# Moving the halves of weights and activations to other byte remainders in a two-block transformer kernel

## The chip, the cores and the metric

The kernel runs on one core of a Trainium2 chip. The metric is the device time of one execution in microseconds (us); the profile is one such execution. The engines are named as in the profile: PE is the matrix engine (its weight loads are listed apart as PEld), DVE the vector engine, ACT the scalar engine, POOL GpSimd, and SP the engine that issues most transfers.

## The reference

Two blocks follow each other on one sequence of 256 tokens with 1024 channels; block 1 has a context of another 256 tokens beside it.

```python
# block 1, two layers: x and ctx
x = sandwich_ffn(x, ...); ctx = sandwich_ffn(ctx, ...)      # gate/up 1024 -> 2 x 2816, silu, down
out_x, out_c = token_mix(hx, hc, w_in, w_out, ...)          # attention + pooling
x = x + gate * rms_norm(out_x); ctx likewise
x = sandwich_ffn(x, ...); ctx = sandwich_ffn(ctx, ...)      # no ctx in the last layer's second half
# block 2, four layers: mixers gla, mla, conv, gla
h = mixer(x)
x = layer_norm(ALPHA * x + h)
x = layer_norm(ALPHA * x + square(relu(x @ w1)) @ w2)       # 1024 -> 4096 -> 1024
x = x + sigmoid(x @ ple_w_gate) * (p @ ple_w_proj)
```

Everything is float32.

## The kernel before

**Products.** Each float32 operand is split exactly into two float32r halves, hi and lo. `mm3` forms one product of two split operands by three matmuls (L180, L181, L182: hi hi, then hi lo, lo hi). `halves` (from L161) makes the halves of weights: the raw weights of a transfer (tile `raw`, 128 x 2048, three buffers) go through one ACT copy (L169, `whi`) and one DVE subtraction (L170, `wlo`), 128 x 1024 at a time, into rings of four buffers each. `split` (L174, L175) does the same for activations.

There are two ways to multiply. `gemm_rows` keeps 128 x 128 activations stationary and moves weights of 512 columns (down projections, `mix_in`, `mix_out`, `mlp` second half, `m_out`, `ple`). `gemm_cols` keeps 128 x 128 weights stationary and moves the activations of all tokens: 512 columns where x and ctx are worked together (`ffn` with `ns == 2`, three of the four feed-forwards of block 1), 256 columns where there is x alone (`ffn` with `ns == 1`, the last feed-forward of block 1; `mlp_hidden`, `gla`'s `project` and `conv` in block 2). Each weight half of 1024 columns serves eight blocks of 128, so 24 matmuls in a row read the same pair of buffers. In the feed-forwards with `ns == 2` the first four pairs are taken over 256 columns at a time.

**Order.** The engines work in the order in which the code emits instructions, moved by priorities (`sooner`, `later`). Transfers of weights go out on SP's queue, three ahead. Steps that form the modulation vectors (`mod_units`, DVE sums) are emitted between the products of the feed-forwards.

**Places in memory.** All tiles lie in the on-chip memory behind each other: pools in the order in which they are opened, tags in the order of first use, each buffer rounded up to 32 bytes. An address here is the byte offset within a partition; its remainder by 512 is what the change speaks of.

| tile | first byte | remainder by 512 |
|---|---|---|
| `whi`, four buffers of 4096 bytes | 51808 | 96, each |
| `wlo`, four buffers of 4096 bytes | 68192 | 96, each |
| block 1: `hT_hi`, `hT_lo` (and `pcat`) | 96992, 113376 | 224 |
| block 1: `hid_hi`, `hid_lo` | 168672, 191200 | 224 |
| block 2: `xT_hi`, `xT_lo`, two buffers each | 84576, 92768, 100960, 109152 | 96 |
| block 2: `mlp_hi`, `mlp_lo` | 159328, 192096 | 96 |
| block 2, mla alone: `cT_hi`, `cT_lo` | 162592, 166688 | 288 |

A block of 128 weights is 512 bytes, a row of 256 columns 1024, a row of 512 columns 2048. So every slice that a matmul of 128 x 128 weights reads has its tile's remainder. One product differs: in mla a weight of 64 columns (`wk`) has slices 256 bytes apart, so its slices stand at 96 and 352 in turn, against `xT` at 96. [...]

**The start.** `rows` (three small transfers) is transposed to `cols`; ACT writes silu of it into `sil`, 128 x 8 x 32 with zeros beyond the first two columns, which is the stationary operand of the first products of the modulation (L323, `mod_pair`). The DVE sums take single columns of `sil` as scalars.

Of the kernel before, what the change touches and what calls it, by code (L numbers as in the profile page):

```python
# [18 lines left out]
P = 128  # L19
# [4 lines left out]
SOONER = 60  # L24
DFF2 = 4096
# [11 lines left out]
def _constants():  # L37
    """Arrays that depend on shapes alone."""
    c = {}
    c["ident"] = np.eye(P, dtype=np.float32)  # L40
    c["one_col"] = np.repeat(np.array([0, 1], np.float32), 64)[:, None]
    inv = np.float32(10000.0) ** (-np.arange(16, dtype=np.float32) / np.float32(16))
    t = np.arange(256)
    tab = np.zeros((2, 2, 256, 2, 16), np.float32)
    for half, pos in enumerate((t // 64, t % 64)):
        ang = pos.astype(np.float32)[:, None] * inv
        tab[0, 0, :, half] = np.cos(ang)
        tab[0, 1, :, half] = np.sin(ang)
    tab[1] = tab[0]
    tab[0] *= np.float32(0.125)  # L50
    c["rope"] = np.ascontiguousarray(
        tab.reshape(2, 2, 2, P, 32).transpose(3, 0, 2, 1, 4).reshape(P, 256))
    j = np.arange(64)
    start = np.clip(j - 8, 0, 48)
    ok = (j[None] >= start[:, None]) & (j[None] < start[:, None] + 16)
    c["na_mask"] = np.tile(np.where(ok, 0.0, NEG).astype(np.float32), (2, 1))

    def pool_matrix(n):
        out = []
        for w in (2, 4, 8, 16):  # L60
            i = np.arange(n)
            lo = np.clip(i - w // 2, 0, n)
            hi = np.clip(i - w // 2 + w, 0, n)
            a = ((i[None] >= lo[:, None]) & (i[None] < hi[:, None])) / (hi - lo)[:, None] - np.eye(n)
            out.append(a.T)
        return np.array(out, np.float32)

    a64 = pool_matrix(64)
    ax = np.zeros((4, P, P), np.float32)
    ax[:, :64, :64] = a64  # L70
    ax[:, 64:, 64:] = a64
    c["pool_x"] = np.ascontiguousarray(ax.transpose(1, 0, 2).reshape(P, 512))
    c["pool_c"] = np.ascontiguousarray(
        pool_matrix(256).reshape(4, 2, P, 256).transpose(2, 1, 0, 3).reshape(P, 2048))
    s = np.arange(P)
    mats, masks = [], [np.eye(P, dtype=bool)]
    for b in (2, 4, 8, 16, 32, 64, 128):
        blk = s // b
        mid = blk * b + b // 2
        up = s >= mid  # L80
        m = np.zeros((P, P), bool)
        for tt in range(P):
            if up[tt]:
                m[mid[tt]:tt + 1, tt] = True
            else:
                m[tt + 1:mid[tt], tt] = True
        mats.append(m)
        if b < 64:
            masks.append((blk[:, None] == blk[None]) & (up[:, None] != up[None]))
    mats.insert(0, s[:, None] > s[None])  # L90
    mats.append(s[:, None] <= s[None])
    c["gla_lev"] = np.concatenate(mats, axis=1).astype(np.float32) / np.float32(16)
    c["gla_mask"] = np.tile(np.concatenate([m[:64, :64] for m in masks], axis=1).astype(np.int32), (2, 1))
    inv2 = np.float32(10000.0) ** (-np.arange(0, 32, dtype=np.float32) * np.float32(2.0 / 64))
    c["mla_inv"] = np.tile(inv2.astype(np.float32), (P, 1))
    return c


class Net:
# [38 lines left out]
    def fbank(self):  # L138
        """Either kind of bank in turn."""
        self.turn = not self.turn  # L140
        return self.bank() if self.turn else self.xbank()
# [19 lines left out]
    def halves(self, v, shape=None, tag=""):  # L161
        """The exact split of v into two float32r parts."""
        kn, cn = v.shape[1], v.shape[2]
        out = []
        for nm in ("hi", "lo"):
            t = self.w.tile([P, 1024], F32R, tag="w" + nm + tag, name="w" + nm, bufs=self.SPL)
            out.append(t[:, :kn * cn].rearrange("p (k c) -> p k c", k=kn))
        hi, lo = out
        self.nc.scalar.copy(hi, v)  # L169
        self.nc.vector.tensor_sub(lo, v, hi.bitcast(F32))  # L170
        return hi, lo
# [5 lines left out]
    def mm3(self, ps, a, b, first, last):  # L177
        """ps += a^T b with both as (hi, lo) pairs."""
# [5 lines left out]
    def gemm_cols(self, ps, w, x, c0, cn):  # L184
        """ps[feature, token] over all k: w hi/lo [P, k, 128], x hi/lo [P, k, tokens]."""
# [5 lines left out]
    def gemm_rows(self, w, kn, c0, cn, x, tiles, per=4, major=2, order=None, bank=None):  # L191
        """Banks [token, column] for each tile; w is a DRAM matrix with kn k-tiles.

        The last major loads are taken tile by tile, so that the first tiles end early."""
# [23 lines left out]
    def rstd_of(self, ms, eps):  # L218
        """(ms + eps)^-1/2; eps may be a column."""
# [10 lines left out]
    def rstd_of_two(self, ms):  # L230
        """The same from the two halves' mean squares."""
# [4 lines left out]
    def meansq(self, src, n):  # L236
        """The sum of squares over n, a power of four."""
# [5 lines left out]
    def columns(self, rows, n, pool, name):  # L243
        """[n, 128] rows -> [128, n]."""
# [6 lines left out]
    def to_columns(self, rows, hi, lo, c0, nblk):  # L251
        """rows: list of tiles [P, nblk*128]; hi/lo [P, block, token] at c0 get the transposes."""
# [13 lines left out]
    def block1(self):  # L266
        nc, tc, d = self.nc, self.tc, self.d
        with ExitStack() as ctx:
# [6 lines left out]
            rows = self.act.tile([24, P], F32, name="rows")  # L275
# [5 lines left out]
            self.sil = self.act.tile([P, KD, 32], F32, name="sil")  # L281
            nc.vector.memset(self.sil, 0.0)
            for s in range(2):
                nc.scalar.activation(self.sil[:, :, s], cols[:, 8 * s:8 * s + 8], AF.Silu)
            self.one_col = self.load_const("one_col", self.act)
# [8 lines left out]
            self.na_mask = self.load_const("na_mask", self.act)  # L294
            self.tail = None
# [13 lines left out]
    def mod_raw(self, l, v, k0):  # L309
        """Rows of k-tiles k0, k0+1 for vector v."""  # L310
# [3 lines left out]
    def mod_pair(self, l, v):  # L314
        """Vectors v and v+1 by matrix products; bank rows 32j (x) and 32j+1 (ctx) for half j."""
# [3 lines left out]
        for k in range(KD):  # L319
            raw = self.load(self.d["w_mod"][l, k * P:(k + 1) * P, v * D:(v + 2) * D]  # L320
                            .rearrange("p (o c) -> p o c", o=1), 1, 2 * D)
            for j in range(4):
                nc.tensor.matmul(acc[32 * j:32 * j + 32, :], lhsT=self.sil[:, k, :],  # L323
# [7 lines left out]
    def mod_units(self, l, vectors):  # L331
        """Steps that form the vectors by sums on the vector engine over k, then over partitions."""
# [36 lines left out]
    def mod_finish(self, l, acc, rows):  # L369
        """From the bank rows (row, vector, half, stream): + b_mod, (1 + scale) g, gate g."""  # L370
# [44 lines left out]
    def modulated(self, l, i, groups):  # L415
        """hT hi/lo [P, 8, tokens] of the modulated norm i for groups of token tiles, each after its tail."""
# [38 lines left out]
    def sooner(self, on=True):  # L455
        """Puts a chain that others wait for ahead of the products around it."""
        return self.tc.high_priority(offset=SOONER) if on else ExitStack()

    def later(self, by):
        """Lets products fill what the chains emitted after them leave free."""  # L460
        return self.tc.high_priority(offset=-by)

    def add_normed(self, t, y, ms):
        """x += y * rstd, y already times the gate row."""
# [4 lines left out]
    def ffn(self, l, w, ns):  # L469
# [25 lines left out]
        with self.tc.tile_pool(name="hid", bufs=1) as hp:  # L495
            self.hp = hp
            for part in range(2):
                hid = tuple(hp.tile([P, HALF_F, 512], F32R, tag="h" + nm, name="hid_" + nm) for nm in ("hi", "lo"))
                for f0 in range(0, HALF_F, 2):
# [7 lines left out]
                    work = [(self.fbank(), h) for h in pre or self.gate_up(l, w, part * HALF_F + f0, fn)]  # L507
# [36 lines left out]
    def gate_up_rows(self, l, w, hT, hid):  # L544
        """Blocks 0 and 1 token by token, so that tile 0 goes ahead."""
# [17 lines left out]
    def gate_up(self, l, w, f0, fn):  # L563
        """The split gate and up columns of blocks f0..f0+fn, in turn."""
        wgu = self.d["w_ffn_gate_up"][l, w]
        raws = [self.load_cols(wgu, c + f0 * P, fn * P) for c in (0, DFF)]
        return [self.halves(r[:, :, f * P:(f + 1) * P]) for f in range(fn) for r in raws]
# [94 lines left out]
    def stacks(self, hp, mp, q, k):  # L662
        """Heads 2hp and 2hp+1 on partitions: q as (hi, lo), (lo, hi) and k as hi twice; k's lo parts in place."""
# [26 lines left out]
    def attend(self, l, s, hp, mp, stacks, vu, cat):  # L690
        """Heads 2hp and 2hp+1 of stream s: local and context keys for x, context keys for ctx."""
# [30 lines left out]
    def softmax_T(self, sc, nk, scale, mp, dst):  # L722
        """Softmax over the free axis of sc, transposed in blocks into dst [P, nk, 128]."""
# [19 lines left out]
    def na_bias(self, l, hp, t, mp):  # L743
        """[P queries, head, 256 keys]: rpb laid out over the window, -1e30 outside it."""
# [78 lines left out]
    def rows_to_xT(self, t, b0, b1, x):  # L823
        """Blocks b0..b1 of token tile t into x."""
# [16 lines left out]
    def layer_norm(self, i, j, gemm):  # L841
        """x = norm(ALPHA x + gemm); returns x transposed, hi/lo."""
# [29 lines left out]
    def mlp_hidden(self, i, hp, x):  # L872
        """relu(x w1)^2 transposed, hi/lo; the first columns token by token, so that tile 0 goes ahead."""
# [13 lines left out]
        for f in range(4, 32, 2):  # L887
            raw = self.load_cols(d["mlp_w1_2"][i], f * P, 256)
            ps = self.bank()
            for e in range(2):  # L890
                w = self.halves(raw[:, :, e * P:(e + 1) * P])
# [4 lines left out]
    def ple_in(self, i):  # L896
        """The transposed per-layer input, hi/lo."""
# [13 lines left out]
    def ple(self, i, pe, x, last):  # L911
        """x += sigmoid(x w) * pe; returns the new x transposed, or stores it."""
# [18 lines left out]
    def gla(self, j, mp, x):  # L931
# [27 lines left out]
        def project(c):  # L959
            raw = self.load_cols(w_in, 256 * c, 256)  # L960
            ps = self.bank()
            for e in range(2):
                self.gemm_cols(ps[:, e * 256:e * 256 + 256], self.halves(raw[:, :, e * P:(e + 1) * P]), x, 0, 256)
# [28 lines left out]
        def scores(h):  # L992
            """Decayed scores of head h [key, query] within each tile and across the two."""
# [102 lines left out]
    def rotate(self, dst, src, cs, t, nh, mp):  # L1096
        """dst, src [P, nh*64]."""
# [14 lines left out]
    def mla(self, j, mp, x):  # L1112
# [23 lines left out]
        def rope_key():  # L1136
            """The rotated key part of all heads, twice over the partitions."""
# [23 lines left out]
        def up(raws, off, width):  # L1161
            """hi/lo [P, 8 heads, width] of the head columns at off, for both k-tiles."""
# [41 lines left out]
        def scores(h):  # L1204
            """The softmax of head h, keys on partitions."""
# [41 lines left out]
    def conv(self, j, mp, x):  # L1247
# [6 lines left out]
        for f0 in range(0, KD, 2):  # L1254
            raws = [self.load_cols(w_in, D * e + f0 * P, 256) for e in range(3)]
            for f in range(2):
                fb = f0 + f
                ps = []
                for e in range(3):
                    b = self.bank()  # L1260
                    self.gemm_cols(b[:, :256], self.halves(raws[e][:, :, f * P:(f + 1) * P]), x, 0, 256)
# [56 lines left out]
```

## Time and profile before

| | |
|---|---|
| median of three runs | 3044.11 us (3041.87 to 3045.15) |
| profiled execution, span | 3045.1 us |
| PE busy | 2980.0 us, 98% |
| DVE busy | 1875.6 us, 62% |
| ACT busy | 1281.8 us, 42% |
| instructions | 40666 |

The span runs from the first to the last instruction. A matmul's duration in the trace is longer than the distance from its start to the next one's start, since matmuls are pipelined: what a matmul costs is read from starts, or from how many fall into a stretch.

### The profile page before, as it was taken

The numbers are of one execution on the slowest core, as the hardware profiler recorded it, in microseconds if no ns is written. First come the engines' busy times: TensorE is split into PE (matmuls) and PEld (weight loads), VectorE is DVE, ScalarE is ACT, GpSimd is POOL, SyncE is SP. The second block draws the span as 40 slices with busy tenths as digits, with TensorE's granted clock in tenths as the row PEclk, the third lists the DMA queues.
The fourth block names the chain that finished last, engine by engine and source line by source line (L and its number), as shares of the span: only waits on it lengthen the run. The fifth ranks groups of instructions, "written<-read, shape, count | busy, mean of one in ns | idle before, by whom it ended". The sixth has DMA issues, their size and how long they took to land.

```text
span 3045.1 us, 40666 instructions
## 1 busy us (share of the span) xinstructions
PE 2980.0 (98%) x16362; PEld 2481.3 (81%) x16362; DVE 1875.6 (62%) x2454; ACT 1281.8 (42%) x1876; POOL 288.6 (9%) x480
## 2 busy tenths in 40 slices
PE   7999999999999999999999999999999999999999
PEld 5777777787778877787789888987798989887997
DVE  5757765577553775336655567656664776467755
ACT  3222245442222422224654465546453545355543
POOL 2101030011110110001100121000000000002000
PEclk9999999999999999999999999999999999999999
DMA  7555531245543454333345536554455565553654
GB/s 280 179 175 180 187 107 63 91 155 180 170 132 110 149 181 154 99 98 120 97 160 186 176 130 192 187 181 165 131 184 187 183 201 183 186 194 111 198 180 145
DMA packets 321936, 484.70 MB, mean 159 GB/s; under 512 B 16606, under 2 KB 199442, under 8 KB 320340
## 3 DMA queue, kind: packets, MB, share of 16 engines
q1 hardware_dynamic: 307844, 461.75, 46.2%
q0 software_dynamic: 9296, 16.16, 1.6%
q10 hardware_dynamic: 4608, 4.20, 0.5%
q8 instruction: 128, 2.10, 0.3%
q14 instruction: 60, 0.49, 0.0%
HBM read 480.97 MB, written 1.10 MB: 158 GB/s over the span
## 4 chain that ended last, share of the span: by engine, by line
PE 89%; DVE 5%; POOL 2%; ACT 2%; DMA 1%; issue 1%; SPq 0%; ACTq 0%; DVEq 0%; POOLq 0%
PE ffn_gu L180 9%; PE ffn_gu L182 9%; PE ffn_gu L181 9%; PE mlp L181 7%; PE mlp L180 7%; PE mlp L182 7%; PE ffn_dn L182 4%; PE ffn_dn L181 4%; PE ffn_dn L180 4%; PE m L180 3%; PE m L182 3%; PE m L181 3%; DVE wlo L170 2%; PE mix_in L181 1%; PE mix_in L180 1%; PE mix_in L182 1%
## 5 line engine op out<-in xcount | busy, mean ns | idle before, releaser
L170 DVE TENSOR_TENSOR wlo<-raw,whi 128x1024 fp32r<-128x1024 f32 (+1 forms) x735 | 884.9, 1211 | 636.6 <-ACT whi L169 621.6
L169 ACT CAST whi<-raw 128x1024 fp32r<-128x1024 f32 (+1 forms) x735 | 760.7, 1038 | 1129.9 <-PE ffn_gu L181 290.7
L181 PE MATMUL ffn_gu<-hT_lo,whi 128*128 128x512 f32 (+1 forms) x1472 | 524.5, 357 | 1.8 <-DVE hT_lo L175 1.8
L180 PE MATMUL ffn_gu<-hT_hi,whi 128*128 128x512 f32 (+1 forms) x1472 | 525.7, 358 | 0.5 <-ACT hT_hi L174 0.5
L182 PE MATMUL ffn_gu<-hT_hi,wlo 128*128 128x512 f32 (+1 forms) x1472 | 523.8, 356 | 0.7 <-DVE wlo L170 0.7
L180 PEld LDWEIGHTS ffn_gu<-hT_hi,whi 128*128 128x128 f32 x1472 | 277.7, 189 | 52.9 <-ACT whi L169 4.2
L181 PEld LDWEIGHTS ffn_gu<-hT_lo,whi 128*128 128x128 f32 x1472 | 278.1, 189 | 43.8 <-DVE hT_lo L175 2.4
L182 PEld LDWEIGHTS ffn_gu<-hT_hi,wlo 128*128 128x128 f32 x1472 | 277.8, 189 | 43.7 <-DVE wlo L170 1.3
L347 DVE SCALAR_TENSOR_TENSOR macc<-raw,sil,macc 128x1024 f32<-128x1024 f32 x224 | 274.6, 1277 | 42.9 <-DMA raw<-in_w_mod_dram 42.9
L180 PE MATMUL mlp<-xT_hi,whi 128*128 128x256 f32 x896 | 253.9, 283 | 0.0
L181 PE MATMUL mlp<-xT_lo,whi 128*128 128x256 f32 x896 | 253.8, 283 | 0.0
L182 PE MATMUL mlp<-xT_hi,wlo 128*128 128x256 f32 x896 | 253.5, 283 | 0.0
L180 PE MATMUL ffn_dn<-whi,hid_hi 128*128 128x512 f32 x616 | 244.1, 396 | 0.0
L181 PE MATMUL ffn_dn<-wlo,hid_hi 128*128 128x512 f32 x616 | 243.6, 395 | 0.0
L182 PE MATMUL ffn_dn<-whi,hid_lo 128*128 128x512 f32 x616 | 243.5, 395 | 0.0
L180 PE MATMUL mlp<-whi,mlp_hi 128*128 128x512 f32 x512 | 199.2, 389 | 0.0
L181 PE MATMUL mlp<-wlo,mlp_hi 128*128 128x512 f32 x512 | 199.2, 389 | 0.0
L182 PE MATMUL mlp<-whi,mlp_lo 128*128 128x512 f32 x512 | 199.2, 389 | 0.0
L181 PEld LDWEIGHTS mlp<-xT_lo,whi 128*128 128x128 f32 x896 | 172.0, 192 | 0.0
L182 PEld LDWEIGHTS mlp<-xT_hi,wlo 128*128 128x128 f32 x896 | 172.0, 192 | 0.0
L180 PEld LDWEIGHTS mlp<-xT_hi,whi 128*128 128x128 f32 x896 | 172.0, 192 | 0.0
L180 PEld LDWEIGHTS ffn_dn<-whi,hid_hi 128*128 128x128 f32 x616 | 115.9, 188 | 29.3 <-ACT yrow L489 2.5
(402 smaller groups left out, 4794.5 us busy)
## 6 DMA issues: line engine op xcount, KB each, us to landing
raw<-in_mlp_w_dram SPq DMA_DIRECT2D x128, 1024.0 KB, 5.4
raw<-in_w_ffn_gate_up_dram SPq DMA_DIRECT2D x80, 1024.0 KB, 5.3
raw<-in_w_mod_dram SPq DMA_DIRECT2D x72, 1024.0 KB, 5.2
raw<-in_w_ffn_down_dram SPq DMA_DIRECT2D x32, 1024.0 KB, 5.1
raw<-in_gla_w_in_dram SPq DMA_DIRECT2D x24, 1024.0 KB, 5.2
raw<-in_w_in_dram SPq DMA_DIRECT2D x16, 1024.0 KB, 5.0
raw<-in_ple_w_gate_dram SPq DMA_DIRECT2D x16, 1024.0 KB, 5.2
raw<-in_w_ffn_down_dram SPq DMA_DIRECT2D x16, 768.0 KB, 4.6
```

The source lines that it names most:

```text
L169: self.nc.scalar.copy(hi, v)
L170: self.nc.vector.tensor_sub(lo, v, hi.bitcast(F32))
L180: mm(ps, lhsT=a[0], rhs=b[0], start=first, stop=False)
L181: mm(ps, lhsT=a[0], rhs=b[1], start=False, stop=False)
L182: mm(ps, lhsT=a[1], rhs=b[0], start=False, stop=last)
L347: nc.vector.scalar_tensor_tensor(acc[s], raw[:, k - k0, :], c, acc[s], ALU.mult, ALU.add)
```

## The change

- `halves` allocates tiles of 1024 + 64 columns in place of 1024. Each buffer of `whi` and `wlo` is 256 bytes longer, so the four buffers of a ring start at remainders 96, 352, 96, 352; both rings turn together. The optional parameters `shape` and `tag`, which no call used, go; a parameter `skew` comes, by which the halves start that many elements into the tile.
- `SKEW = 16` elements, 64 bytes, is given in the `gemm_cols` products with 256 columns of `ffn` with `ns == 1`, `mlp_hidden`, `gla`'s `project`, and `conv`. There the weights start at remainder 160 or 416.
- `rows` goes from the pool `act` into a buffer of `tmp`; `sil` shrinks to 128 x 8 x 2, and its wide form with zeros is a buffer of `tmp` (`gp`), filled by a DVE copy. Together with `even(80)`, a tile of 320 bytes that POOL fills with zeros, this moves `hT` to 97888 and 114272 and `hid` to 169568 and 192096: remainder 96. Block 2's tiles move by 2048 bytes and keep their remainders. The highest byte in use becomes 228960.

Comments and docstrings are emptied throughout; those lines are left out here.

```diff
+SKEW = 16
...
+    def even(self, n):
+        self.nc.gpsimd.memset(self.act.tile([P, n], F32, name="even"), 0.0)
...
-    def halves(self, v, shape=None, tag=""):
+    def halves(self, v, skew=0):
         kn, cn = v.shape[1], v.shape[2]
         out = []
         for nm in ("hi", "lo"):
-            t = self.w.tile([P, 1024], F32R, tag="w" + nm + tag, name="w" + nm, bufs=self.SPL)
-            out.append(t[:, :kn * cn].rearrange("p (k c) -> p k c", k=kn))
+            t = self.w.tile([P, 1024 + 64], F32R, tag="w" + nm, name="w" + nm, bufs=self.SPL)
+            out.append(t[:, skew:skew + kn * cn].rearrange("p (k c) -> p k c", k=kn))
...
-            rows = self.act.tile([24, P], F32, name="rows")
+            rows = self.tmp.tile([P, 512], F32, tag="hf", name="rows", bufs=3)[:24, :P]
...
-            self.sil = self.act.tile([P, KD, 32], F32, name="sil")
-            nc.vector.memset(self.sil, 0.0)
+            self.sil = self.act.tile([P, KD, 2], F32, name="sil")
+            wide = self.tmp.tile([P, D], F32, tag="gp", name="wide")
+            self.wide = wide[:, :KD * 32].rearrange("p (k s) -> p k s", k=KD)
+            nc.vector.memset(self.wide, 0.0)
             for s in range(2):
                 nc.scalar.activation(self.sil[:, :, s], cols[:, 8 * s:8 * s + 8], AF.Silu)
+            nc.vector.tensor_copy(self.wide[:, :, 0:2], self.sil)
...
             self.na_mask = self.load_const("na_mask", self.act)
+            self.even(80)
...
-                nc.tensor.matmul(acc[32 * j:32 * j + 32, :], lhsT=self.sil[:, k, :],
+                nc.tensor.matmul(acc[32 * j:32 * j + 32, :], lhsT=self.wide[:, k, :],
...
-                    work = [(self.fbank(), h) for h in pre or self.gate_up(l, w, part * HALF_F + f0, fn)]
+                    work = [(self.fbank(), h) for h in pre or self.gate_up(l, w, part * HALF_F + f0, fn,
+                                                                           SKEW if ns == 1 else 0)]
...
-        return [self.halves(r[:, :, f * P:(f + 1) * P]) for f in range(fn) for r in raws]
+        return [self.halves(r[:, :, f * P:(f + 1) * P], skew) for f in range(fn) for r in raws]
...
-                w = self.halves(raw[:, :, e * P:(e + 1) * P])
+                w = self.halves(raw[:, :, e * P:(e + 1) * P], SKEW)
```

The same third argument is added in `project` of `gla` and in `conv`.

## Rows read from the trace of the kernel before

**Rows 1.** The page: busy time, granted clock by slices, the chain that ended last.
```profile
PE 2980.0 (98%) x16362; PEld 2481.3 (81%) x16362; DVE 1875.6 (62%) x2454; ACT 1281.8 (42%) x1876; POOL 288.6 (9%) x480
...
PEclk9999999999999999999999999999999999999999
...
PE 89%; DVE 5%; POOL 2%; ACT 2%; DMA 1%; issue 1%; SPq 0%; ACTq 0%; DVEq 0%; POOLq 0%
```

**Rows 2.** Waits of PE, longest in total first: us, times, longest.
```profile
PE mod L323 <- DMA raw<-in_w_mod_dram: 11.8, 8, 2.9
PE ffn_t L440 <- DVE yrow L428: 6.8, 8, 1.7
```

**Rows 3.** Matmuls by line and shape: count | busy us, mean ns.
```profile
L180 PE MATMUL ffn_gu<-hT_hi,whi 128*128 128x512 f32 x960 | 380.3, 396 | 0.0
...
L180 PE MATMUL mlp<-xT_hi,whi 128*128 128x256 f32 x896 | 253.9, 283 | 0.0
...
L180 PE MATMUL ffn_dn<-whi,hid_hi 128*128 128x512 f32 x616 | 244.1, 396 | 0.0
...
L180 PE MATMUL mlp<-whi,mlp_hi 128*128 128x512 f32 x512 | 199.2, 389 | 0.0
...
L180 PE MATMUL ffn_gu<-hT_hi,whi 128*128 128x256 f32 x512 | 145.4, 285 | 0.5 <-ACT hT_hi L174 0.5
...
L180 PE MATMUL m<-xT_hi,whi 128*128 128x256 f32 x320 | 91.5, 287 | 1.1 <-ACT whi L169 1.1
...
L180 PE MATMUL mix_in<-whi,hT_hi 128*128 128x512 f32 x224 | 89.9, 407 | 0.0
...
L180 PE MATMUL mix_out<-whi,pcat_hi 128*128 128x512 f32 x84 | 34.0, 405 | 0.0
```

**Rows 4.** Stretches of one kind of matmul: us, busy time of each engine (count), clock, DMA.
```profile
1230.00:1330.00 100.00, 100.00 (x432) 81.06 (x431) 33.55 (x36) 28.31 (x36) 1.92 (x4) 1.00 0.33 102
1340.00:1390.00 50.00, 50.00 (x216) 40.23 (x215) 19.15 (x22) 12.95 (x23) 6.78 (x11) 1.00 0.24 82
1640.00:1697.00 57.00, 57.00 (x483) 57.00 (x482) 32.72 (x41) 26.96 (x40) 0.00 (x0) 1.00 0.61 199
1965.00:2047.00 82.00, 82.00 (x364) 67.91 (x363) 40.89 (x40) 31.17 (x30) 0.62 (x1) 1.00 0.56 186
1886.00:1962.00 76.00, 76.00 (x636) 76.00 (x635) 47.76 (x52) 40.62 (x53) 0.00 (x0) 1.00 0.58 183
2400.00:2460.00 60.00, 60.00 (x503) 60.00 (x502) 42.87 (x70) 26.41 (x36) 0.00 (x0) 1.00 0.60 197
2108.60:2112.40 3.80, 3.80 (x36) 3.80 (x35) 3.80 (x10) 1.87 (x4) 0.00 (x0) 1.00 0.00 0
2091.30:2093.30 2.00, 2.00 (x20) 2.00 (x19) 1.23 (x2) 0.68 (x3) 1.49 (x2) 1.00 0.74 311
```

**Rows 5.** PE in order of time, block 1, first feed-forward: start us, duration us.
```profile
100.29 0.40 PE L181 MATMUL ffn_gu<-hT_lo,whi 128*128 128x512 f32 x1
100.53 0.40 PE L182 MATMUL ffn_gu<-hT_hi,wlo 128*128 128x512 f32 x1
100.77 0.39 PE L180 MATMUL ffn_gu<-hT_hi,whi 128*128 128x512 f32 x1
```

**Rows 6.** PE in order of time, mla's values in block 2, first and last of eleven.
```profile
2104.21 0.39 PE L180 MATMUL m<-whi,cT_hi 128*128 128x512 f32 x1
...
2106.49 0.39 PE L181 MATMUL m<-wlo,cT_hi 128*128 128x512 f32 x1
```

**Rows 7.** All engines in order of time, the start.
```profile
4.09 0.18 DVE L248 COPY cols<-init_t 128x24 f32<-128x24 f32 x1 [2.93 <-PE init_t L246]
4.31 0.31 ACT L284 ACTIVATE sil<-cols 128x8 f32<-128x8 f32 x2 [2.29 <-DVE cols L248]
...
6.95 1.93 PE L323 MATMUL mod<-raw,sil 128*32 128x512 f32 x8 [2.90 <-DMA raw<-in_w_mod_dram]
```

**Rows 8.** Transposes on PE by line and shape, in block 1 and in block 2.
```profile
L740 PE MATMUL mix_att_t<-ident,pr 128*128 128x128 f32 x160 | 25.4, 276 | 0.0
...
L828 PE MATMUL m_out_t<-ident,xr 128*128 128x128 f32 x64 | 9.2, 276 | 1.2 <-DVE xr L868 1.1
```

More of the change, by code (lines that the diff above doesn't have):

```diff
@@ L561, in gate_up_rows, with gate_up @@
             self.to_columns([sg], hid[0], hid[1], t * P, 2)
-    def gate_up(self, l, w, f0, fn):
+    def gate_up(self, l, w, f0, fn, skew=0):
         wgu = self.d["w_ffn_gate_up"][l, w]
         raws = [self.load_cols(wgu, c + f0 * P, fn * P) for c in (0, DFF)]
-        return [self.halves(r[:, :, f * P:(f + 1) * P]) for f in range(fn) for r in raws]
+        return [self.halves(r[:, :, f * P:(f + 1) * P], skew) for f in range(fn) for r in raws]
     def rope_rows(self, b, row, c, t, mp):
@@ L962, in project @@
             for e in range(2):
-                self.gemm_cols(ps[:, e * 256:e * 256 + 256], self.halves(raw[:, :, e * P:(e + 1) * P]), x, 0, 256)
+                self.gemm_cols(ps[:, e * 256:e * 256 + 256], self.halves(raw[:, :, e * P:(e + 1) * P], SKEW), x, 0, 256)
             h0 = 2 * (c % 2)
@@ L1260, in conv @@
                     b = self.bank()
-                    self.gemm_cols(b[:, :256], self.halves(raws[e][:, :, f * P:(f + 1) * P]), x, 0, 256)
+                    self.gemm_cols(b[:, :256], self.halves(raws[e][:, :, f * P:(f + 1) * P], SKEW), x, 0, 256)
                     ps.append(b)
```

## The prediction

> **What bounds the kernel now.** [...] Then PE's waits: the largest is 11.8 us for the first transfers of `mod_pair`, the next 6.8 us [rows 2]. So no wait is left that is worth a per cent; what could move the time is the step from one matmul to the next. The lines by shape give counts, but their mean durations overlap [rows 3]. Therefore I took stretches in which PE does one kind of matmul without a gap and divided: stretch plus one duration (a matmul that began just before the stretch counts too), by the count [rows 3, 4]. PE is busy through all of each, the clock is 1.00, and DVE, ACT and DMA have slack in all but the short seventh [rows 4].
>
> | stretch [rows 4] | what | remainders: weights, activations | ns a matmul |
> |---|---|---|---|
> | 1230 to 1330 | block 1 gate/up, 512 columns | 96, 224 | 100.40/432 = 232.4 |
> | 1340 to 1390 | block 1 down, 512 | 96, 224 | 50.40/216 = 233.3 |
> | 1965 to 2047 | block 2 `mlp` second half, 512 | 96, 96 | 82.39/364 = 226.3 |
> | 1640 to 1697 | block 1 gate/up, 256 | 96, 224 | 57.28/483 = 118.6 |
> | 1886 to 1962 | block 2 `mlp` first half, 256 | 96, 96 | 76.28/636 = 119.9 |
> | 2400 to 2460 | block 2 conv, 256 | 96, 96 | 60.28/503 = 119.8 |
> | 2108.6 to 2112.4 | block 2 mla heads, 256 | 96, 288 | 4.08/36 = 113.3 |
> | 2091.3 to 2093.3 | mla `wk`, 64 weights, 256 | 96 and 352, 96 | 2.28/20 = 114.0 |
>
> [...] In block 1 both ways of multiplying give the same pace, weights stationary or moving. The quietest stretch (DVE 33.55 of 100 us, DMA share 0.33) is slow, and the block 2 stretch with DVE at 40.89 of 82 and DMA at 0.56 is fast. Matmuls with 512 columns at a distance of 192 (mla values) lie between: 2.28 us for ten steps, 228 ns [rows 6]. The fast mla heads differ from `mlp`'s first half mainly in where their activations lie.
>
> [...]
>
> **The change part by part.**
>
> *Block 1, 512 columns, distance 128 to 0.* After the change `hT` and `hid` stand at 96, the weights at 96 or 352 in turn. Counts for each of the three lines: 960 gate/up, 616 down, 224 `mix_in` [rows 3] and 96 `mix_out` (by its loops; the row with `pcat` holds 84). Three lines make 2880, 1848, 672 and 288, 5688 in all. At block 2's 226.3 ns: gate/up 2880 x 6.1 = 17.6 us, down 1848 x 7.0 = 12.9, the two mixer parts 960 x 6.1 = 5.9; together 36.4 us. PE has no gap there, so all of it shortens the span. This price is known for the buffers at 96. For those at 352 it isn't: no product of 128 weights in the trace has operands 256 apart. The nearest row is `wk`, whose slices alternate between 96 and 352 against 96; 114.0 ns is the mean over both, and one of them slower by 6.7 ns would give a mean of at least 116.7 were the other at 113.3 [rows 4]. So a distance of 256 seems to act like 0 there, though with half as many weights to load. I take it so. Bounds: for the buffers at 352, the same 226.3 below, and above 240 ns, the longest step in block 1's pattern [rows 5].
>
> *Block 2, 512 columns.* 1020 a line by the loops, 512 of them in the row of `mlp` [rows 3], 3060 in all. Half of them will have weights 256 away from the activations, where all had 0. By the same reading nothing changes; if 256 acts like the worst 128, 1530 x 6.6 = 10.1 us are lost.
>
> *256 columns with `SKEW`.* 896 and 320 a line [rows 3], 3648 in block 2, and of the 512 a line in block 1 the 320 with `ns == 1` (twenty blocks, two weights, eight slices), 960. Activations at 96, weights at 160 or 416: activations minus weights is -64 or -320. By 512, -320 is the +192 of the mla heads, which ran at 113.3; -64 is the same place if the pattern repeats every 256 bytes, as `wk` suggests. I take 113.3 for both: 3648 x (119.9 - 113.3) = 24.1 us and 960 x (118.6 - 113.3) = 5.1 us. [...] What feeds PE keeps up: 48 matmuls use one transfer of 1 MB in 5.44 us, which is what 24 at 226.3 ns already do in the second half of `mlp`; DVE would be busy 47.76 of some 71.8 us [rows 4].
>
> *256 columns without `SKEW`* (the first pairs with `ns == 2`): 192 a line, 576; distance 128 becomes 0 or 256, 118.6 to 119.9: a loss of 0.7 us.
>
> *The start.* One DVE copy is added behind silu. `cols` took 0.18 us; silu ends at 4.62 and the first product waits for its weights until 6.95 [rows 7], 2.3 us of cover. Without it the price is 0.2 us. `even` is one POOL memset of 80 columns, behind POOL's transfers of constants, which nothing on PE awaits. `rows` and the wide zeros use buffers that are free by then. Nothing.
>
> *Other matmuls.* Transposes in block 1 see their rows move by 128 against the identity. They average 276 ns in both blocks, at different distances [rows 8]; nothing.
>
> The sum: 36.4 + 24.1 + 5.1 - 0.7 = 64.9 us off the span, 3045.1 - 64.9 = 2980.2. The profiled execution's span is 1.0 us above the median of the runs, so the median to expect is 2979 us, 2.1% less.
>
> **The rivals.**
>
> *A, the forecast:* distances repeat every 256 bytes, 2979 us. Its own range is 2970 to 2992: each 512 pace may be 1 ns off (5.7 us), and the groups of 24 may need a few matmuls each to fall into step.
>
> *B, half of it:* the pattern repeats only every 512 bytes, and the larger tiles put half of the weights at the wrong place. Then half of 36.4 and of 29.2 is gained (32.8), 10.1 is lost in block 2 and 0.7 at the first pairs: 22.0, so 3022 us at the median. For it speaks that only buffers at 96 have a price in the trace; against it `wk`. A mere loss of either of the two large parts (36.4 or 29.2) ends between A and B as well.
>
> *C, the change doesn't do what it says:* the paces belong to the stages (shapes, banks, other engines), not to the remainders, and the time stays at 3044. For it speaks that no stage was seen at two remainders; against it the agreement of quite different stages at the same ones. [...]
>
> *D, slower:* 256 apart is a worse place than any seen. Its place is every product without `SKEW` whose weights lie at 352: 2844 in block 1 and 1530 in block 2. The rest gains half of 36.4 and 29.2 less 0.7, 32.1 us. With X ns for these products the loss is 2844 (X - 232.7) + 1530 (X - 226.3), 232.7 being block 1's mean; it eats the gain from X = 237.8. At 240, the longest step shown [rows 5], it is 20.8 + 21.0 = 41.8, and the median is 3054. For it: nothing in the trace excludes it; against it: `wk`, and that the pace at 128 has already a mean of only 232.7.
>
> **How the numbers follow.** A 0.60, B with what lies between 0.23, C 0.09, D 0.08. The predicted time is A's, 2979. Holding A and most of B leaves out about 2 in 10: 2970 to 3026. A and B are faster by over 0.2% (6 us, about what a measurement of this kernel can tell from no change): 0.83. C is within it, 0.09. D is slower, 0.08.
>
> **What would show it.** Same stages, same division. Block 1 gate/up and down at 226 to 227 ns a matmul, for both parities of weights; `mlp`'s first half, conv and the last feed-forward at 113 to 114; the second half of `mlp` still at 226 to 227. Under B, groups of 24 matmuls alternate between two paces with the buffers; under C nothing moves; under D the second half of `mlp` becomes slower than 232. PE's share of the span stays at 98%. I am wrong if the remainder isn't the cause, or if a distance of 256 isn't equal to 0.

## The result and the profile after

The changed kernel takes 2990.84 us in the median (2986.48 to 2993.78, four runs) against 3042.99 us before (3040.04 to 3045.15): a ratio of 0.9828, 95% interval 0.9815 to 0.9841. 2979 us was forecast, the range was 2970 to 3026; 52.2 of the 64.9 us came.

The page of the changed kernel (engine busy times; the chain that ended last), against [rows 1]:

```profile
PE 2924.5 (98%) x16362; PEld 2457.6 (82%) x16362; DVE 1875.6 (63%) x2455; ACT 1280.5 (43%) x1876; POOL 288.3 (10%) x481
...
PE 87%; DVE 6%; DMA 2%; ACT 2%; POOL 2%; issue 1%; SPq 0%; ACTq 0%; DVEq 0%; POOLq 0%
```

The same 16362 matmuls keep PE busy for 55.5 us less; DVE's busy time is the same 1875.6 us. So the gain lies in the step from one matmul to the next. The stretches that answer to [rows 4] (columns as there; matmuls per stretch in the second column):

```profile
1230.00:1300.00 70.00, 70.00 (x310) 57.99 (x309) 24.48 (x27) 20.42 (x26) 0.00 (x0) 1.00 0.31 102
1310.00:1350.00 40.00, 40.00 (x178) 33.11 (x178) 14.14 (x17) 10.08 (x17) 2.85 (x4) 1.00 0.30 99
1535.00:1575.00 40.00, 40.00 (x356) 40.00 (x355) 23.64 (x30) 20.15 (x30) 0.00 (x0) 1.00 0.61 200
1610.00:1668.00 58.00, 58.00 (x495) 58.00 (x494) 33.69 (x42) 27.46 (x42) 0.00 (x0) 1.00 0.61 196
1855.00:1925.00 70.00, 70.00 (x597) 70.00 (x596) 44.98 (x49) 37.79 (x49) 0.00 (x0) 1.00 0.60 190
1930.00:2010.00 80.00, 80.00 (x355) 66.30 (x355) 39.59 (x36) 31.68 (x31) 0.00 (x0) 1.00 0.55 185
2160.00:2228.00 68.00, 68.00 (x603) 68.00 (x602) 45.02 (x50) 38.95 (x50) 0.00 (x0) 1.00 0.62 196
2360.00:2410.00 50.00, 49.85 (x440) 49.65 (x439) 33.94 (x58) 21.11 (x29) 0.00 (x0) 1.00 0.56 180
2460.00:2530.00 70.00, 70.00 (x597) 70.00 (x596) 44.48 (x49) 38.88 (x50) 0.00 (x0) 1.00 0.60 189
2800.00:2868.00 68.00, 68.00 (x579) 68.00 (x579) 43.95 (x49) 37.43 (x49) 0.00 (x0) 1.00 0.59 187
```

Divided as in the prediction:

| stage | ns before [rows 4] | ns after |
|---|---|---|
| block 1 gate/up, 512 columns | 232.4 | 70.39/310 = 227.1 |
| block 1 down, 512 | 233.3 | 40.39/178 = 226.9 |
| `mlp` second half, 512 | 226.3 | 80.39/355 = 226.5 |
| last feed-forward, first part, 256 | 44.28/369 = 120.0 | 40.28/356 = 113.1 |
| last feed-forward, second part, 256 | 118.6 | 58.28/495 = 117.7 |
| `mlp` first half of layer 1, 256 | 119.9 in layer 0 | 68.28/603 = 113.2 |
| the same of layers 0, 2 and 3 | 119.9 in layer 0 | 117.7, 117.7, 117.9 |
| conv, 256 | 119.8 | 50.28/440 = 114.3, with 0.15 us of gaps |

One row of before is new here, the first part of the last feed-forward:

```profile
1560.00:1604.00 44.00, 44.00 (x369) 44.00 (x368) 24.83 (x32) 20.15 (x30) 0.00 (x0) 1.00 0.57 188
```

One matmul more or less in a stretch moves such a quotient by 0.2 ns where some 600 are counted, and by over 1 ns in the shortest stretches here. Where that matters, paces below are means of the steps from one start to the next in the timeline, and are said to be "by starts". By starts, 512 columns at the remainders 96 and 96 take 226.7 ns in block 2 of both kernels and in block 1 of the changed one, and the two paces of the matmuls with `SKEW` are 113.3 and 117.8 ns.

Matmuls with 512 columns came to the pace that was forecast. Those with 256 columns split: the same code, the same remainders and the same shapes run at 113.2 in one layer and at 117.7 in the next. Nothing in the prediction speaks of that, though the kernel before had a sign of it: the two parts of the last feed-forward stood at 120.0 and 118.6 with the same remainders.

Whether weights at 352 differ from those at 96 is seen in four stretches of 5.44 us, the time of one group of 24 matmuls at 226.7 ns, one behind the other in block 1's gate/up of the changed kernel, where consecutive groups read buffers at 96 and 352 in turn (us, PE busy, count, clock, DMA):

```profile
1230.00:1235.44 5.44, 5.44 (x25) 1.00 0.58 193
1235.44:1240.88 5.44, 5.44 (x25) 1.00 0.62 193
1240.88:1246.32 5.44, 5.44 (x25) 1.00 0.00 0
1246.32:1251.76 5.44, 5.44 (x25) 1.00 0.00 0
```

Every group has the same 25. Distances of 0 and 256 take the same pace here. "Distance" is used below for the first byte of the moving operand minus that of the stationary one, modulo 256.

### The profile page after: what moved, and what is told of

Its sections match the earlier page's. It is cut to its first block, busy times and chain, and to the rows that moved or that the text cites. A ratio compares the mean times of both kernels' runs of the same rounds, so it can differ in the third digit from the quotient of the medians.

```text
span 2992.0 us, 40671 instructions
## 1 busy us (share of the span) xinstructions
PE 2924.5 (98%) x16362; PEld 2457.6 (82%) x16362; DVE 1875.6 (63%) x2455; ACT 1280.5 (43%) x1876; POOL 288.3 (10%) x481
## 4 chain that ended last, share of the span: by engine, by line
PE 87%; DVE 6%; DMA 2%; ACT 2%; POOL 2%; issue 1%; SPq 0%; ACTq 0%; DVEq 0%; POOLq 0%
PE ffn_gu L185 9%; PE ffn_gu L187 9%; PE ffn_gu L186 9%; PE mlp L185 7%; PE mlp L186 7%; PE mlp L187 7%; PE ffn_dn L187 4%; PE ffn_dn L186 4%; PE ffn_dn L185 4%; PE m L185 2%; PE m L186 2%; PE m L187 2%; DVE wlo L175 2%; PE mix_in L186 1%; PE mix_in L185 1%; PE mix_in L187 1%
```

## The experiments

Theory 1 is the prediction's: the pace goes by the distance modulo 256. Its rivals are a pattern of 512 bytes, the stage itself, and the place in the tile.

**The two parts by themselves.** Block 1's alignment without the skew:

```diff
-SKEW = 16
+SKEW = 0
```

> The change with SKEW 0: larger tiles and block 1's activations at 96, weights at 96 or 352, nothing skewed. Theory 1 (the pace of a matmul goes by the distance of activations and weights, modulo 256): 512 columns in block 1 stay at 227 ns for both parities of weights, all matmuls with 256 columns are at 119.9 to 120.2, also in the mla stage's neighbours; against the changed kernel some 4608 matmuls lose 3 to 6 ns, 16 to 22 us, so about 3010 us. Rival (the skew has no part in it, the larger tiles do the work in the 256-column stages): those stages keep 113 to 118 ns and the time stays near 2991.

Measured: 3011.06 us (3009.04 to 3013.52), ratio to before 0.9899, interval 0.9881 to 0.9917. Its stretches of gate/up, last feed-forward, `mlp` first half and conv (columns as above):

```profile
1230.00:1300.00 70.00, 70.00 (x310) 57.99 (x309) 24.46 (x27) 20.42 (x26) 0.00 (x0) 1.00 0.32 102
1612.00:1668.00 56.00, 56.00 (x469) 56.00 (x468) 31.30 (x39) 26.44 (x40) 0.00 (x0) 1.00 0.62 201
1856.00:1928.00 72.00, 72.00 (x602) 72.00 (x601) 45.00 (x50) 38.87 (x50) 0.00 (x0) 1.00 0.59 187
2368.00:2425.00 57.00, 57.00 (x478) 57.00 (x476) 40.76 (x68) 25.16 (x34) 0.00 (x0) 1.00 0.60 200
```

227.1 ns with 512 columns, and 120.0, 120.1 and 119.8 with 256. The larger tiles alone do nothing for the latter; the rival falls. This part is worth 31 us of the 52.

The skew without the alignment:

```diff
-            self.even(80)
+            self.even(112)
```

> The change with block 1's activations put back to remainder 224 by a larger filler tile. Theory 1: 512 columns in block 1 at 232 to 233 ns again for weights at 96 and at 352 alike, which costs about 31 us against the changed kernel; block 2's 256 columns as in the changed kernel, 113 or 118 ns; about 3022 to 3028 us. The last feed-forward of block 1 has a distance of +64 here, whose pace no run has shown. Rival (a pattern of 512 bytes): weights at 352 and at 96 show two different paces in block 1, group by group.

Measured: 3019.61 us (3015.91 to 3021.86), ratio 0.9926, interval 0.9904 to 0.9948, below the 3022 to 3028 us expected. Gate/up, last feed-forward, `mlp` first half of layer 0 and conv:

```profile
1232.00:1330.00 98.00, 98.00 (x423) 79.45 (x423) 32.47 (x35) 27.55 (x35) 1.53 (x4) 1.00 0.32 102
1642.00:1697.00 55.00, 55.00 (x470) 55.00 (x468) 31.77 (x40) 25.74 (x39) 0.00 (x0) 1.00 0.63 205
1886.00:1954.00 68.00, 68.00 (x602) 68.00 (x601) 45.01 (x50) 38.95 (x50) 0.00 (x0) 1.00 0.61 197
2385.00:2440.00 55.00, 55.00 (x469) 55.00 (x469) 37.95 (x65) 22.88 (x33) 0.00 (x0) 1.00 0.55 178
```

232.6 ns with 512 columns; behind the first, its groups of 24 lie between 232.1 and 232.8 ns by starts, so the weights at 96 and at 352 share one pace here too. Here `mlp` of layer 0 has 113.4 and conv 117.9, the other way round than in the changed kernel, and block 2's places are the same in both. So the places do not decide between the two paces.

**Other distances.** Four kernels vary `SKEW` and the filler tile; block 1 and block 2 get different distances in each. The diff is scan a's. Scans b, c and e have `SKEW` 48, 8 and 24 and a filler of 64, 88 and 72; in the last feed-forward, where the code has `SKEW if ns == 1 else 0`, scans b and e put 0, and scan c 32 in place of `SKEW`.

```diff
-SKEW = 16
+SKEW = 32
...
-            self.even(80)
+            self.even(96)
```

Scan a:

> Distances (activations minus weights) varied: block 1's 512 columns at +64, block 2's 256 columns at -128 (SKEW 32), the last feed-forward at -64 by another pair of places (160 against 224). Theory 1: the last feed-forward shows the paces of the changed kernel, 113 or 118 ns, since only the distance counts; -128 gives the 118.6 to 120 that +128 gave before; +64 with 512 columns lies between, about 229, as the values of mla at -192 did. Rival (the place itself counts, not the distance): the last feed-forward is at 120.

Scan b:

> Distances varied: block 1's 512 columns at -64, the last feed-forward at -64 without any skew of its weights (32 against 96), block 2's 256 columns at -192, which is +64 modulo 256 (SKEW 48). Theory 1: the last feed-forward is at 113 or 118 ns without a skew. 512 columns at -64 and 256 columns at +64 have no row yet; if distances +64 and -64 are alike, 256 columns are at 113 to 118 and 512 at about 229. Rival (the skew inside the tile counts): the last feed-forward is at 120 and block 2 alone gains.

Scan c:

> Half steps: block 2's 256 columns at -32 (SKEW 8), the last feed-forward at -96, block 1's gate/up with 512 columns at +32 and down at -32 (moving minus stationary). Theory 1 with lines of 64 bytes as its grain: -32 acts like 0 or like -64, so 120, 118 or 113; 512 columns act like 0 or like +64, 227 or 230, and like 0 or -64, 227 or 234. Rival (finer grain): paces not seen so far, in between.

Scan e:

> Half steps, the other side: block 2's 256 columns at -96 (SKEW 24), the last feed-forward at -32 without skew, block 1's gate/up at -32 and down at +32. Grain of 64 bytes: -96 acts like -64 or -128, so 113, 118 or 119; the last feed-forward as block 2 in the other half-step run; gate/up and down exchange their paces against that run. Rival (finer grain): others.

They took 3026.69, 3025.9, 3034.89 and 3032.26 us, one run each. Gate/up, down, last feed-forward and `mlp` first half, of scan a and then of scan b:

```profile
1222.00:1315.00 93.00, 93.00 (x408) 76.28 (x408) 32.29 (x35) 26.68 (x34) 1.56 (x4) 1.00 0.31 98
1328.00:1375.00 47.00, 47.00 (x203) 37.67 (x202) 16.48 (x19) 10.85 (x18) 4.05 (x6) 1.00 0.30 101
1630.00:1682.00 52.00, 52.00 (x461) 52.00 (x460) 30.97 (x39) 25.62 (x38) 0.00 (x0) 1.00 0.63 205
1870.00:1942.00 72.00, 72.00 (x609) 72.00 (x609) 45.65 (x50) 39.06 (x51) 0.00 (x0) 1.00 0.60 190
```

```profile
1226.00:1320.00 94.00, 94.00 (x405) 75.73 (x404) 31.74 (x34) 26.77 (x34) 1.29 (x3) 1.00 0.29 96
1334.00:1380.00 46.00, 46.00 (x202) 37.75 (x201) 16.47 (x19) 10.86 (x18) 4.05 (x6) 1.00 0.29 101
1634.00:1686.00 52.00, 52.00 (x461) 52.00 (x460) 30.90 (x39) 25.63 (x38) 0.00 (x0) 1.00 0.64 209
1874.00:1945.00 71.00, 71.00 (x605) 71.00 (x604) 45.33 (x51) 38.91 (x50) 0.00 (x0) 1.00 0.60 189
```

In the first pairs (the 256-column products at the start of a feed-forward with both streams) no weights are skewed, so their distance is gate/up's. Those of scan a are at +64: the first feed-forward's, then the second one's. Behind them stands `mlp` of layer 2 in scan e, at -96.

```profile
50.00:62.00 12.00, 12.00 (x108) 12.00 (x108) 11.76 (x15) 6.45 (x10) 0.00 (x0) 1.00 0.43 133
639.00:654.00 15.00, 15.00 (x129) 15.00 (x129) 13.65 (x16) 8.10 (x11) 0.00 (x0) 1.00 0.42 141
```

```profile
2495.00:2565.00 70.00, 70.00 (x593) 70.00 (x592) 44.69 (x49) 37.57 (x49) 0.00 (x0) 1.00 0.60 187
```

12.28/108 = 113.7 and 15.28/129 = 118.4 ns (113.3 and 117.8 by starts), and 70.28/593 = 118.5 ns. With the same stretches of scans c and e the paces by distance are, in ns:

| distance | 512 columns | 256 columns |
|---|---|---|
| 0 | 227.1 (gate/up), 226.9 (down) | 119.8 to 120.1 |
| +32 | 233.4 (gate/up, c), 233.8 (down, e) | 116.7 by starts (first pairs, c) |
| -32 | 233.6 (gate/up, e), 233.3 (down, c) | 118.3 (`mlp`, c), 118.4 (last ffn, e) |
| +64 | 228.9 (gate/up, a), 229.7 (down, b); one down stretch of b 233.3 by starts | 117.6 (last ffn, skew alone), 117.8 (`mlp`, b); 113.3 and 117.8 by starts (first pairs, a) |
| -64 | 233.1 (gate/up, b), 233.4 (down, a) | 113.2 and 117.8 (changed kernel), 113.4 (last ffn, a and b) |
| -96 | not run | 117.3 (`mlp` of layer 0, e), 117.4 (last ffn, c); 118.5 (`mlp` of layer 2, e) |
| 128 | 232.6 (skew alone), 232.4 and 233.3 (before) | 118.7 (`mlp`, a, at -128), 118.6 and 120.0 (before) |

Gate/up, which keeps the weights stationary, and down, which moves them, take the same pace within 1 ns at the same distance, and exchange it between scans a and b (228.9 and 229.7 ns at +64, 233.1 and 233.4 at -64). The last feed-forward runs at 113.4 ns in both, at 160 against 224 and at 32 against 96, once with and once without a skew. So it is the distance, not the stage and not the place in the tile. The grain is finer than 64 bytes: with 512 columns +32, at 233.4 and 233.8 ns, is as bad as 128, at 232.4 to 233.3, where 0 takes 227.1. At -64, 512 columns did not take the 229 that scan b's expectation guessed from likeness to +64, and scan a's "-128 gives 118.6 to 120" held.

Two paces at one distance are not peculiar to -64: +64, -96 and 128 show two each in this table. At 0 every stretch of every run has one, 226.7 or 120.0 ns by starts, and at -32 and +32 no second one was seen.

**What decides between 113 and 118.** The changed kernel was run again, the code the same.

> The changed kernel once more, word for word but for the order of two assignments. Seen so far at a distance of -64 or +64 with 256 columns: a whole stage runs either at 113.3 or at 117.9 ns. Theory L (which of the two a stage takes hangs on the few ns with which it is entered): the choice differs between this profile and the first one in at least one of the nine stages, and single runs lie some 3 us apart per stage. Rival (the choice is fixed by the program): the same stages at 117.9 (mlp of layers 0, 2 and 3, second part of the last feed-forward), the same at 113.3.

Measured: 2990.22 us (2987.7 to 2994.36), ratio 0.9826, interval 0.9809 to 0.9843. Second part of the last feed-forward, `mlp` of layers 0, 1, 2, 3, conv:

```profile
1610.00:1668.00 58.00, 58.00 (x495) 58.00 (x494) 33.44 (x41) 27.33 (x42) 0.00 (x0) 1.00 0.62 200
1855.00:1920.00 65.00, 65.00 (x576) 65.00 (x575) 43.53 (x49) 37.15 (x49) 0.00 (x0) 1.00 0.62 195
2156.00:2222.00 66.00, 66.00 (x585) 66.00 (x584) 43.86 (x48) 37.87 (x49) 0.00 (x0) 1.00 0.62 196
2458.00:2526.00 68.00, 68.00 (x602) 68.00 (x601) 45.43 (x50) 39.04 (x50) 0.00 (x0) 1.00 0.61 194
2795.00:2863.00 68.00, 68.00 (x579) 68.00 (x579) 43.90 (x48) 37.57 (x49) 0.00 (x0) 1.00 0.60 186
2352.00:2410.00 58.00, 58.00 (x495) 58.00 (x494) 41.53 (x69) 25.75 (x35) 0.00 (x0) 1.00 0.61 200
```

117.7, 113.3, 113.3, 113.4, 117.9 and 117.7 ns: layers 0 and 2 are fast this time, conv is slow. So the program alone does not make the choice. This profile is from another chip than the next one, so that a chip has its own choice was still open. A third time, on the chip of the next comparison:

> The changed kernel once more, for the comparison on one chip. Theory L: again about half of the nine stages with 256 columns at 113.3 and half at 117.9 ns, in another choice than in the two profiles so far; median 2988 to 2993 us, single runs up to 8 us apart.

Measured: 2987.14 us (2983.69 to 2993.49), ratio 0.9816, interval 0.9798 to 0.9833, just below the median expected. Three of the nine stages are slow, and in conv the pace changes within the stage, with the program, the chip and the execution the same. Two stretches of 10 us, and between them, from PE in order of time, the only gap:

```profile
2390.00:2400.00 10.00, 10.00 (x91) 10.00 (x90) 6.13 (x11) 3.36 (x5) 0.00 (x0) 1.00 0.94 310
2405.00:2415.00 10.00, 10.00 (x88) 10.00 (x87) 6.68 (x12) 3.62 (x5) 0.00 (x0) 1.00 0.80 283
```

```profile
2402.16 0.39 PE L185 MATMUL m<-xT_hi,whi 128*128 128x256 f32 x1 [0.44 <-ACT c_sb L1276]
```

Before the gap 10.28/91 = 113.0 ns, after it 10.28/88 = 116.8 by this short count, 113.3 and 117.8 by starts. PE waited 0.44 us once and came back at the other pace. That a gap draws the pace anew is what this one case suggests. It need not change it: in the first profile of the changed kernel PE waited at the same matmul, for 0.2 us, and conv held 113.3 ns before and 113.5 after, by starts.

**A mixture.** The author's guess, which no run shows, was that the slow pace is a state in which every weight load meets the matmul beside it in the same way; then loads of two kinds may not hold it. Hi halves stay at 16 elements, lo halves go to 48:

```diff
-            out.append(t[:, skew:skew + kn * cn].rearrange("p (k c) -> p k c", k=kn))
+            o = skew if nm == "hi" else (64 - skew) % 64
+            out.append(t[:, o:o + kn * cn].rearrange("p (k c) -> p k c", k=kn))
```

> The changed kernel with the lo halves of skewed weights at 48 elements in place of 16: hi halves at distance -64, lo halves at +64. Theory L with the state between neighbours: a weight load meets the matmul before it, and now the loads of a group don't all meet alike, so the slower of the two states may not hold: all stages with SKEW at 113.3, some 12 us less than the changed kernel where that took 117.9 in four of nine. Rival: the mixture holds neither, 118 to 120 throughout.

One run, 2988.56 us, without the 12 us expected; every stage with skew at 113 to 114 ns. One run says little of its time, and in its mla stage, which has no skew, the granted clock was 0.61 over 20 us (us, PE busy, count, clock, DMA).

```profile
2080.00:2100.00 20.00, 18.17 (x59) 0.61 0.20 71
```

Timed:

> The lo halves of skewed weights at 48 elements, the hi halves at 16, timed. Theory L: the slow state does not hold with loads of two kinds; all nine stages at 113.3 ns in this profile as well, and about half of the 4608 matmuls gain 4.6 ns against the changed kernel: 8 to 12 us less, 2979 to 2984 us. Rival (the first such profile was luck): some stages at 117.9, and the time that of the changed kernel.

Measured: 2982.33 us (2980.04 to 2987.7), as expected; ratio to before 0.9803, interval 0.9785 to 0.982. Second part of the last feed-forward and `mlp` of layers 2 and 3, slow in at least one profile of the changed kernel:

```profile
1612.00:1664.00 52.00, 52.00 (x461) 52.00 (x460) 30.95 (x39) 25.80 (x39) 0.00 (x0) 1.00 0.62 204
2452.00:2520.00 68.00, 68.00 (x603) 68.00 (x602) 45.29 (x50) 38.96 (x50) 0.00 (x0) 1.00 0.62 196
2788.00:2855.00 67.00, 67.00 (x593) 67.00 (x593) 44.53 (x49) 38.88 (x50) 0.00 (x0) 1.00 0.61 196
```

113.4, 113.2 and 113.5 ns. Last, the same in the two places that had been left out:

```diff
-            pre = self.gate_up(l, w, 0, 2)
+            pre = self.gate_up(l, w, 0, 2, SKEW)
...
-                                                                           SKEW if ns == 1 else 0)]
+                                                            SKEW if ns == 1 or part == f0 == 0 else 0)]
...
-            return [self.halves(raw[:, 0, :].rearrange("p (h c) -> p h c", h=8)[:, :, off:off + width])
+            return [self.halves(raw[:, 0, :].rearrange("p (h c) -> p h c", h=8)[:, :, off:off + width],
+                                lo=32 if off == 0 else None)
```

Here `lo` is a new argument of `halves`, the offset of the lo half alone.

> The kernel with hi and lo apart, and the same in two more places: the first pairs of the feed-forwards with both streams (576 matmuls, 256 columns, 120 ns so far) and mla's heads (192 matmuls, 113 or 118 ns). Theory 1: the first pairs at 113 to 114, 576 x 6.4 = 3.7 us less, mla's heads at 113.3 always, some 0.4 us; 2975 to 2980 us. Rival: the first pairs are not bound by this step, since other engines feed them at the start of a feed-forward, and nothing comes of it.

Measured: 2980.29 us (2978.06 to 2984.86), just above the range expected; ratio 0.9795, interval 0.9778 to 0.9813. The first pairs, in this kernel:

```profile
51.00:62.00 11.00, 11.00 (x99) 11.00 (x98) 11.00 (x14) 6.21 (x10) 0.00 (x0) 1.00 0.45 139
```

11.28/99 = 113.9 ns, though DVE is busy throughout. The second half of mla's heads takes 113.3 ns by starts, against 117.8 in the profile without this step; that is one profile each, and other profiles had 113.3 there without it. On this one chip the changed kernel's median is 2987.14, with hi and lo apart 2982.33, with the two places 2980.29. The intervals of the three ratios overlap, so that the last two beat the changed kernel rests on the medians and on the paces: of twenty-seven stages in three profiles the changed kernel showed eleven slow ones and one that changed within, these kernels none in three profiles. The draw isn't even: the second part of the last feed-forward and the `mlp` of layer 3 were slow in all three profiles of the changed kernel, the first part and the `mlp` of layer 1 fast in all.

## Why the prediction was right, and where it was off

*That the remainders make the paces* was right. The same products at other addresses move by up to 6.7 ns by starts (120.0 to 113.3). Rivals B, C and D fall: no group differs by parity (25 matmuls in each 5.44 us), one and the same stage changes its pace with the remainders (gate/up 232.4 to 227.1 ns), and a distance of 256 acts like 0 (226.7 ns by starts over both).

The 16362 matmuls come in the same order in both profiles. So each step, from one start to the next, can be set against its own in the other profile, and the steps can be added up by kind.

*Block 1, 512 columns:* forecast 36.4 us. The steps of gate/up are 16.1 us shorter in sum, those of down 9.9 and those of the mixers 2.1: 28.1. Three sizes were off. The pace after the change, 226.3, came from one count; by starts it is 226.7 there too. Down was priced at the 233.3 of one stretch; others of its stretches stood at 232.3 by starts, the other pace at distance 128. And "PE has no gap there" doesn't hold for the mixers: `mix_in` waited for DVE's `wlo` 3.7 us in four waits before and 4.1 after. The first mixer gave 1.9 us and the second 0.2, of 5.9 forecast; what held back the rest isn't shown. The block's part alone took 31 us off the median.

*Block 2, 512 columns:* unchanged, 226.7 by starts, as forecast.

*256 columns:* the step that failed in size is "I take 113.3 for both". It is right as a pace and not as a certainty: four of nine stages took 117.7. Of 24.1 us forecast for block 2 this profile shows 14.2, and of 5.1 for the last feed-forward 3.3: its first part gained 2.8 and its second 0.5.

*First pairs:* forecast 0.7 us lost. They went from 118.7 ns in two feed-forwards and 120.0 in the third, by starts, to 120.0 in all, but the steps of all 576 add up to the same time within 0.1 us.

*The start* cost nothing: the added copy takes 0.25 us and ends at 4.57, the first product comes at 7.00 in place of 6.95 [rows 7], with the transfer.

These terms add up to 28.1 + 14.2 + 3.3 = 45.6 us, against 64.9 forecast. The spans of the two profiles differ by 3045.1 - 2992.0 = 53.1 us, and most of the other 7.5 is no address at all, but the granted clock. In the mla stage of the profile before it was 0.74 over ten us of which PE was busy for 8.4, and 0.50 over the next ten; the same stage of the profile after held 1.00, with stretches in which PE was busy no more (7.9 of 10 us). Two stretches of before (us, PE busy, count, clock, DMA), then the first product of mla's heads and the first of `m_out`, before and after, in order of time:

```profile
2120.00:2130.00 10.00, 8.42 (x31) 0.74 0.27 97
2130.00:2140.00 10.00, 9.75 (x30) 0.50 0.14 52
```

```profile
2096.81 0.38 PE L180 MATMUL m<-cT_hi,whi 128*128 128x256 f32 x1 [0.68 <-ACT cT_hi L174]
2154.45 0.47 PE L180 MATMUL m_out<-whi,xT_hi 128*128 128x512 f32 x1
```

```profile
2064.04 0.50 PE L185 MATMUL m<-cT_hi,whi 128*128 128x256 f32 x2 [0.68 <-ACT cT_hi L179]
2113.76 0.48 PE L185 MATMUL m_out<-whi,xT_hi 128*128 128x512 f32 x1
```

57.6 us became 49.7, 7.9 less. Against that stands 1.0 us lost before the last feed-forward's skewed products: behind a wait of 3.8 us both profiles have matmuls of 256 columns at 213 ns, in the profile after at a granted clock of 0.51 (1517 to 1520 us), and that profile has ten or so more of them. The rest is 0.6 us.

The mla stage is not faster by the change: in the thirteen profiles of this case it takes 49.7 to 57.9 us, 57.8 in the third one of the changed kernel. So the distance to the forecast was made smaller by luck in this pair of profiles. How much of the 52.2 us between the medians is of this kind isn't shown. That it matters for single executions is: of nine of the kernel before on one chip, two with a mean granted clock of 0.998 took 3034.72 and 3038.26 us, seven with 0.991 to 0.994 took 3044.83 to 3045.82. The clock line of the page [rows 1] has slices of 76 us, in which such 10 us don't show.

## What to carry to other kernels

When one engine is busy for 98% of a kernel, divide stretches by counts: a pace that differs between stages of one shape, as 119.9 and 113.3 ns did here, is work that isn't in any wait. Where stationary and moving operands stand relative to each other, worth up to 6.7 ns of 120.0 in this kernel, can then be tried like a tile size, set with a filler tile or an offset; find its best value for each shape by a scan, since two likenesses failed here: gate/up took 228.9 ns at +64 and 233.1 at -64, and the distance 0, the best for 512 columns at 227.1, took 120.0 with 256, where -64 took 113.3. A pace read from one short stretch may be one of two, as 113.3 and 117.8 ns were here: look at other stretches at the same distance, and at the same stage in several executions, before counting on it. Compare matmul by matmul where the order is the same, so that a change of clock isn't taken for a gain.

## What the runs showed of the hardware

- The step of a float32r matmul with 128 x 128 weights, each loaded for one matmul, went by the distance of its two operands modulo 256 bytes: 227 to 233.8 ns with 512 columns, 113.2 to 120.1 with 256. Weights at 96 and at 352 against activations at 96 took the same: 25 matmuls in each 5.44 us. The best distance seen for 512 columns, 0, is at 120.0 ns the worst seen with 256.
- At a distance of -64 with 256 columns there are two steady paces, 113.3 and 117.8 ns, for the same instructions at the same addresses. Which one holds differed between three profiles, not all from one chip, and once changed within a stage, behind a gap of 0.44 us. Two paces at one distance were also seen at +64 (113.3 and 117.8; 228.9 and 233.3 with 512 columns), -96 (117.3 and 118.7) and 128 (118.7 and 120.0; 232.4 and 233.3), by starts.
- The granted clock fell to 0.50 for 10 us in the mla stage of one execution of the kernel before and to 0.61 over 20 us in one with hi and lo apart, and held 1.00 there in one of the changed kernel. The stage took 57.6, 56.4 and 49.7 us.
- With hi and lo halves at -64 and +64 the slow one of the two was not seen in three profiles. Why is not known: no run shows what the two operands do to each other inside, and the explanation by states is argued from when the pace changes.
